# A ring of seven weight tiles, plain weights split two pairs at a time, and four pairs by seven products

## The chip, the cores and the metric

The kernel runs on one core of a Trainium2 chip. The metric is the device time of one execution in microseconds (us). Five engines work side by side and meet only through semaphores: TensorE (PE, with its weight loads shown as PEld), VectorE (DVE), ScalarE (ACT), GpSimd (POOL) and SyncE (SP), the last of which issues most of the DMA transfers.

## The reference

One decoder block on 256 tokens of width 2048, all in float32:

```python
h = h + 0.5 * swiglu(rms_norm(h, ffn1_norm), ffn1_w_gu, ffn1_w_down)
h = h + hybrid_mixer(rms_norm(h, mix_norm), w_in, ..., w_out)
h = h + 0.5 * swiglu(rms_norm(h, ffn2_norm), ffn2_w_gu, ffn2_w_down)
gate = sigmoid(rms_norm(h, ple_norm) @ ple_w_gate)
h = h + gate * (p @ ple_w_proj)
out = rms_norm(h, final_norm)

def swiglu(x, w_gu, w_down):
    gate, up = split(x @ w_gu, 2)
    return (silu(gate) * up) @ w_down
```

The hidden width of both feed-forward blocks (FFNs) is 5632. The mixer projects to 14 blocks of 512 columns, runs a gated delta rule and a stick-breaking attention on them, and projects back. Only the matrix products with large weights matter here.

## The kernel before

**Split products.** Every large product keeps float32 accuracy by splitting both operands into a high half (rounded to the matmul's input type) and a low half (the rest). A product of a 128x128 piece of the activations with a 128x512 piece of the weights is then three matmuls: high by high, high by low, low by high. Activations stand as the PE's stationary operand, weights move. The weights come from memory whole and are split on the chip: ACT casts the raw tile to the high half (`whi` or `shi`), then DVE subtracts it from the raw tile to give the low half (`wlo` or `slo`).

**Pairs.** The unit of plain work is a pair: two 128-row pieces of weights, 512 columns wide, 512 KB. `weight_pair` (L64) takes a `raw` tile (a ring of 4), a `whi` and a `wlo` tile (rings of 3 each), issues one load on SP's queue, one cast on ACT (L74) and one subtraction on DVE (L75). A pair feeds 12 matmuls (two pieces, two halves of the tokens, three matmuls each).

**Seven products.** Part of each FFN product is done by Strassen's scheme in its seven-product form: a 2x2 arrangement of weight blocks (two output blocks by the two halves of a pair's rows) against the 2x2 arrangement of the two halves of the tokens and of the rows. A `Group` (L245) covers two output blocks: gate and up of one hidden block of 512 columns (kind `gu`), or two blocks of the down projection (`dn`, `nb` 0 and 2), or two blocks of the last gate matrix (`behind`). Of each block's pairs the first `ns` go through the seven products, the others are plain. `ns` is `NS` = 4 for `gu`, `NS_DOWN` for `dn` (2, 3, 3 for the three parts), 2 for `behind`. The seven weight operands are made one after the other by `all_sums` (L287) from four loaded quarters `R`, 128 x (`ns` x 512): cast (L295), subtract (L296), then DVE or an accumulating DMA on POOL's queue (L311) adds the next quarter into `R`. `shi` and `slo` are rings of two. `product` (L324) runs one of the seven, 3 x `ns` matmuls; `halves` (L420) makes the sums and differences of the activations that the products need (`S`, `Sh`, `Sl`).

**Order.** The hidden blocks are worked in three `PARTS`: blocks 0 to 2, 3 to 6 and 7 to 10. For each part come its `gu` groups, then its two `dn` groups over the hidden blocks of this part. In the first FFN two hidden blocks are wholly plain, in the second one. `plan` (L351) writes the order of one FFN as a list: a group's plain pairs, and between them the seven products of the group that follows (from the second pair on where both are of one kind, from the third where they differ), so that the seven operands can be made while PE has other work. In the first `dn` group of a part the plain pairs that read the hidden block finished last stand at the end. All weights, of the mixer and the last stage too, form one list `order`. `next_weights` (L82) is called once for each piece of PE work; it issues splits ahead along that list, up to two pairs beyond the current one (`LEAD`) and up to two products' operands, and hands out the next one. Between pairs `lanes.step` advances small generators (norms, transposes, gating, `halves`).

**A hidden block's way.** `down_input` (L470) multiplies up by the gate's silu on DVE (L477), transposes blockwise (L482, `tb`), stores `tb` to memory and reads it back as `tT` (L488, L493), and splits it into `hTh` and `hTl` (ACT L499, DVE L500). For the last hidden block of a part the steps follow closer (`last`, L573).

**The end.** The last output block of the last gate matrix has its eight pairs split ahead into eight own buffers (L698), and its products run in two halves of the tokens.

The tile framework places each engine's instructions by its own order of readiness, with the program's order as priority; a tile waits until one of its tag's buffers is free.

## Time and profile before

| | us |
|---|---|
| median of 3 runs | 1951.76 |
| lowest, highest | 1951.52, 1951.91 |
| the profiled execution | 1953.25 |
| its span, first to last instruction | 1951.5 |

In the windows quoted below each row gives a stretch of the span and its length, then for PE, PEld, DVE, ACT and POOL the busy time with the number of instructions in brackets, then the granted PE clock, the DMA engines' busy share and what they moved in GB/s. In group rows the numbers behind the count are the total busy time, the mean duration in ns, and the engine's idle time just before the group with what ended it. In timeline rows the first number is the start in us, the second the time that the row covers. Rows of the chain give start, duration and what ran. A DMA issue row ends with the median time from issue to landing.

### The profile page before, as it was taken

How to read it: one execution, taken by the hardware profiler on the slowest of the kernel's cores; microseconds unless marked ns; L12 is line 12 of the kernel's file. 1: busy time of each engine (PE TensorE's matmuls, PEld its weight loads, DVE VectorE, ACT ScalarE, POOL GpSimd, SP SyncE). 2: the span in 40 equal slices, each digit the busy share in tenths (PEclk: the TensorE clock that was granted, in tenths of full speed). 3: DMA queues.
4: the chain of work that ended last, by engine and by line, in shares of the span. 5: the costliest groups of instructions: out<-in, count | busy, mean ns of one | idle time of the engine just before them, and what ended most of it. 6: DMA issues, size and time to landing. Idle time of an engine off the chain costs nothing.

```text
span 1951.5 us, 24163 instructions
## 1 busy us (share of the span) xinstructions
PE 1932.7 (99%) x8884; PEld 1591.6 (82%) x8884; DVE 1567.9 (80%) x1679; ACT 1163.1 (60%) x1358; POOL 148.8 (8%) x226
## 2 busy tenths in 40 slices
PE   9999999999999999999999999999999999999997
PEld 7888888888888888878788888888888788887886
DVE  7889878997889766797856579889888987888965
ACT  6656666566665567664555456566565755656653
POOL 0010100000010000010100000010000100001000
PEclk9999999999999999999999999999999999999999
DMA  8778888788887765556565786888898987988864
GB/s 311 268 238 276 255 288 285 227 293 251 282 283 237 225 216 172 175 169 209 173 201 160 244 289 226 226 285 289 241 282 251 303 266 237 272 255 282 249 208 141
DMA packets 144184, 475.06 MB, mean 243 GB/s; under 512 B 19649, under 2 KB 47297, under 8 KB 129857
## 3 DMA queue, kind: packets, MB, share of 16 engines
q1 hardware_dynamic: 107200, 302.16, 44.4%
q0 software_dynamic: 25920, 160.44, 30.2%
q10 hardware_dynamic: 10944, 10.91, 1.7%
q8 instruction: 69, 1.13, 0.2%
q14 instruction: 51, 0.41, 0.1%
HBM read 451.44 MB, written 22.02 MB: 243 GB/s over the span
## 4 chain that ended last, share of the span: by engine, by line
PE 87%; DVE 6%; DMA 4%; issue 2%; ACT 1%; SPq 0%; POOL 0%; POOLq 0%; DVEq 0%; ACTq 0%
PE g L340 5%; PE d L541 5%; PE d L542 5%; PE g L339 5%; PE d L540 4%; PE g L341 4%; PE u L540 4%; PE u L542 4%; PE u L541 4%; PE g L541 4%; PE g L542 4%; PE pj L109 4%; PE pj L110 4%; PE pj L111 4%; PE g L540 4%
## 5 line engine op out<-in xcount | busy, mean ns | idle before, releaser
L74 ACT CAST whi<-raw 128x1024 fp32r<-128x1024 f32 (+1 forms) x489 | 512.1, 1050 | 427.1 <-PE pj L111 109.9
L75 DVE TENSOR_TENSOR wlo<-raw,whi 128x1024 fp32r<-128x1024 f32 (+1 forms) x489 | 592.0, 1217 | 166.1 <-ACT whi L74 163.8
L296 DVE TENSOR_TENSOR slo<-R,shi 128x2048 fp32r<-128x2048 f32 (+2 forms) x224 | 445.2, 1989 | 149.0 <-ACT shi L295 147.6
L295 ACT CAST shi<-R 128x2048 fp32r<-128x2048 f32 (+2 forms) x224 | 374.2, 1671 | 140.5 <-DVE R L304 62.1
L109 PE MATMUL pj<-whi,nTh 128*128 128x512 f32 x448 | 179.4, 401 | 0.0
L110 PE MATMUL pj<-wlo,nTh 128*128 128x512 f32 x448 | 175.3, 391 | 1.1 <-DVE wlo L75 1.1
L111 PE MATMUL pj<-whi,nTl 128*128 128x512 f32 x448 | 174.9, 390 | 0.0
L541 PE MATMUL d<-wlo,hTh 128*128 128x512 f32 x448 | 174.3, 389 | 0.0
L540 PE MATMUL d<-whi,hTh 128*128 128x512 f32 x448 | 174.2, 389 | 0.0
L542 PE MATMUL d<-whi,hTl 128*128 128x512 f32 x448 | 173.7, 389 | 0.0
L541 PE MATMUL g<-wlo,nTh 128*128 128x512 f32 x400 | 155.9, 390 | 0.4 <-DVE wlo L75 0.4
L541 PE MATMUL u<-wlo,nTh 128*128 128x512 f32 x400 | 155.7, 389 | 0.5 <-DVE wlo L75 0.5
L542 PE MATMUL g<-whi,nTl 128*128 128x512 f32 x400 | 155.8, 390 | 0.0
L542 PE MATMUL u<-whi,nTl 128*128 128x512 f32 x400 | 155.7, 389 | 0.0
L540 PE MATMUL g<-whi,nTh 128*128 128x512 f32 x400 | 155.4, 390 | 0.0
L540 PE MATMUL u<-whi,nTh 128*128 128x512 f32 x400 | 154.2, 389 | 0.2 <-ACT whi L74 0.2
L304 DVE TENSOR_TENSOR R<-R 128x2048 f32<-128x2048 f32 (+2 forms) x68 | 135.7, 1995 | 0.1
L110 PEld LDWEIGHTS pj<-wlo,nTh 128*128 128x128 f32 x448 | 84.2, 188 | 18.9 <-DVE wlo L75 2.7
L111 PEld LDWEIGHTS pj<-whi,nTl 128*128 128x128 f32 x448 | 84.1, 188 | 17.6
L542 PEld LDWEIGHTS d<-whi,hTl 128*128 128x128 f32 x448 | 84.1, 188 | 17.6
L541 PEld LDWEIGHTS d<-wlo,hTh 128*128 128x128 f32 x448 | 84.1, 188 | 17.6
L540 PEld LDWEIGHTS d<-whi,hTh 128*128 128x128 f32 x448 | 84.1, 188 | 17.4
(332 smaller groups left out, 3445.2 us busy)
## 6 DMA issues: line engine op xcount, KB each, us to landing
raw<-in_w_gu SPq DMA_DIRECT2D x199, 512.0 KB, 5.7
raw<-in_w_down SPq DMA_DIRECT2D x112, 512.0 KB, 6.5
raw<-in_w_in SPq DMA_DIRECT2D x112, 512.0 KB, 3.4
R<-in_w_gu2q POOLq DMA_DIRECT2D x54, 1024.0 KB, 8.6
R<-in_w_gu1q POOLq DMA_DIRECT2D x48, 1024.0 KB, 8.6
raw<-in_w_out SPq DMA_DIRECT2D x32, 512.0 KB, 4.2
tT<-scr SPq DMA_DIRECT2D x22, 512.0 KB, 5.1
R<-in_w_down11q POOLq DMA_DIRECT2D x12, 768.0 KB, 6.0
```

Source lines behind the costliest of these rows:

```text
L74: nc.scalar.copy(hi[:, j, :], raw[:, j, :])
L75: nc.vector.tensor_tensor(out=lo[:, j, :], in0=raw[:, j, :], in1=hi[:, j, :], op=ALU.subtract)
L109: nc.tensor.matmul(outs[t], xh[:, c], whi[:, j, :], start=st, stop=False)
L110: nc.tensor.matmul(outs[t], xh[:, c], wlo[:, j, :], start=False, stop=False)
L111: nc.tensor.matmul(outs[t], xl[:, c], whi[:, j, :], start=False, stop=sp)
L295: keep(nc.scalar.copy(hi, w))
L296: nc.vector.tensor_tensor(out=lo, in0=w, in1=hi, op=ALU.subtract)
L304: keep(nc.vector.tensor_tensor(out=self.raw[x], in0=self.raw[x], in1=self.raw[y], op=ALU.add))
L339: nc.tensor.matmul(out, xh, whi[:, g, :], start=st, stop=False, skip_group_check=True)
L540: nc.tensor.matmul(out, xh[:, c], whi[:, j, :], start=st, stop=False, skip_group_check=True)
L541: nc.tensor.matmul(out, xh[:, c], wlo[:, j, :], start=False, stop=False, skip_group_check=True)
L542: nc.tensor.matmul(out, xl[:, c], whi[:, j, :], start=False, stop=sp, skip_group_check=True)
```

## The change

It does four things.

1. `NS_DOWN` becomes (2, 4, 3): the two down groups of the second part, in both FFNs, put four pairs through the seven products. `halves` gets a case for four pairs in a down group (one block of two, two of one), and `last` becomes 2 for this part.
2. The rings `whi`, `wlo` (3 each, one pair) and `shi`, `slo` (2 each, four pairs) become one ring of seven tiles of 128x2048, three in the pool that lives throughout (`w`) and four in the FFN's pool (`f`), in the order `ffwfwfw`. An operand of a product takes two of them, high and low.
3. From the third pair of each FFN up to its end (in the second FFN up to the `behind` group), plain pairs are split as quads: two pairs in one raw tile of 128x2048, loaded by two transfers, one cast and one subtraction, two tiles of the ring. All other plain pairs stay single: high and low side by side in one `w` tile. A quad's tiles are free again when both of its pairs have been used.
4. `raw` becomes a ring of two tiles of two pairs. Single pairs share one by twos, so both are loaded when the first is due. `next_weights` no longer counts pairs ahead; it issues as long as the oldest tiles of the ring that it needs have been used.

```diff
-LEAD = 2
+RING = "ffwfwfw"
+CAP = {x: RING.count(x) for x in "wf"}
...
-NS_DOWN = tuple(3 if i1 - i0 == 4 else 2 for i0, i1 in PARTS)
+NS_DOWN = (2, 4, 3)
...
-        raw = wp.tile([P, 2, NB], F32, tag="raw", name="raw", bufs=4)
-        hi = pool.tile([P, 2, NB], F32R, tag="whi", name="whi", bufs=bufs)
-        lo = pool.tile([P, 2, NB], F32R, tag="wlo", name="wlo", bufs=bufs)
...
+    def new_raw():
+        return wp.tile([P, 4, NB], F32, tag="raw", name="raw", bufs=2)
+
+    def halved(hi, lo, src):
+        nc.scalar.copy(hi, src)
+        nc.vector.tensor_tensor(out=lo, in0=src, in1=hi, op=ALU.subtract)
+
+    def weight_pair(raw, w, parts=1):
+        for i in range(parts):
+            j = slice(2 * i // parts, 2 * (i + 1) // parts)
+            halved(w[:, 0:2][:, j], w[:, 2:4][:, j], raw[:, j])
+        return w[:, 0:2], w[:, 2:4]
+
+    class Pairs:
+        def load(self):
+            if self.raw is None:
+                self.raw = new_raw()
+                n = 2 if done[0] else 1
+                for k in range(0, 2 * len(self.srcs), n):
+                    nc.sync.dma_start(out=self.raw[:, k:k + n], in_=self.srcs[k // 2][:, k % 2:k % 2 + n])
+            return self.raw
+
+    class Op:
+        def issue(self, where):
+            slots = [(wp if x == "w" else current[0]).tile([P, NS, NB], F32R, tag="w", name="w",
+                                                            bufs=CAP[x]) for x in where]
+            if self.kind == "sum":
+                self.out = [self.src.next_operand(*slots)]
+            elif self.kind == "single":
+                raw = self.src.load()[:, 2 * self.at:2 * self.at + 2]
+                self.out = [weight_pair(raw, slots[0], 2 if not done[0] else 1)]
+            else:
+                halved(slots[0], slots[1], self.src.load())
+                self.out = [tuple(x[:, 2 * i:2 * i + 2] for x in slots) for i in range(2)]
...
+    def places(op):
+        if op.kind == "single":
+            return "w"
+        return "".join(RING[(done[2] + i) % len(RING)] for i in range(2))
...
     def next_weights():
-        ahead = max(1, min(LEAD, done[1] // 2))
+        if done[1]:
+            uses[done[1] - 1][0].left -= 1
+        ahead = max(1, done[1] // 2)
...
+            if "f" in where and current[0] is None:
                 break
+            if any(len(ring[x]) + where.count(x) - CAP[x] > sum(not o.left for o in ring[x][:where.count(x)])
+                   for x in "wf"):
+                break
+            if sum(o.left > 0 for o in set(ring["w"] + ring["f"])) > ahead:
+                break
+            op.issue(where)
...
+    def add_plan(n):
+        first = len(order)
+        ffn_plan[n] = plan(n)
+        pairs = [i for i in range(first, behind_at.get(n, len(order))) if order[i][0] == "pair"][2:]
+        quads.update(pairs[:len(pairs) // 2 * 2])
...
-        for g0 in range(0, ns, 2):
-            n = min(2, ns - g0)
+        for g0, n in {1: ((0, 1),), 2: ((0, 2),), 3: ((0, 2), (2, 1)),
+                      4: ((0, 2), (2, 1), (3, 1)) if kind == "dn" else ((0, 2), (2, 2))}[ns]:
...
-                        last = (3 if i1 - i0 == 4 else 2) if len(hTh) == i1 else 0
+                        last = (6 - NS_DOWN[group.part] if i1 - i0 == 4 else 2) if len(hTh) == i1 else 0
...
-        ws = [weight_pair(a["w_pg"][3][g], fp, KD // 2) for g in range(KD // 2)]
+        ws = []
+        for g in range(0, KD // 2, 2):
+            both = Pairs([a["w_pg"][3][g], a["w_pg"][3][g + 1]])
+            for i in range(2):
+                w = fp.tile([P, 4, NB], F32R, tag="w", name="w", bufs=KD // 2)
+                ws.append(weight_pair(both.load()[:, 2 * i:2 * i + 2], w))
```

`next_operand` is the former `all_sums` with its two result tiles handed in. In the list of work (`make_program`) a quad stands at the place of its first pair.

More of the change, by code (lines that the diff above doesn't have):

```diff
@@ L82, in next_weights @@
-    def next_weights():
-        ahead = max(1, min(LEAD, done[1] // 2))
-        while done[0] < len(order):
-            kind, src = order[done[0]]
-            if kind != "load" and sum(k == kind for k, _ in split) > (ahead if kind == "pair" else 1):
-                break
-            done[0] += 1
-            if kind == "load":
-                src()
-            elif kind == "sum":
-                split.append((kind, next(src.sums)))
-            else:
-                split.append((kind, weight_pair(src, parts=2 if not done[1] and not split else 1)))
+            halved(w[:, 0:2][:, j], w[:, 2:4][:, j], raw[:, j])
@@ L96, in next_weights @@
         done[1] += 1
-        return split.pop(0)[1]
+        return op.out[i]
     def accumulate(outs, xs, nk):
@@ L265, in __init__ @@
                 self.plain.sort(key=lambda x: x[1] // 2)
-            self.sums = self.all_sums()
+            self.given = 0
         def new_banks(self):
@@ L399, in plan @@
             todo = []
+            if group.kind == "behind":
+                behind_at[n] = len(order)
             for j, (b, g) in enumerate(group.plain):
```

116 lines of the change are left out of this document (81 added, 35 removed).

## The prediction

> **What bounds the kernel now.** I read the page's engine shares first, then the chain that ended last, then busy time by windows, and last the single stretches in which PE isn't full.
>
> ```profile
> span 1951.5 us, 24163 instructions
> PE 1932.7 (99%) x8884; PEld 1591.6 (82%) x8884; DVE 1567.9 (80%) x1679; ACT 1163.1 (60%) x1358; POOL 148.8 (8%) x226
> PE 87%; DVE 6%; DMA 4%; issue 2%; ACT 1%; SPq 0%; POOL 0%; POOLq 0%; DVEq 0%; ACTq 0%
> ...
> 0.00:20.00 20.00, 18.25 (x77) 14.93 (x78) 13.34 (x23) 12.36 (x18) 0.79 (x7) 1.00 0.85 290
> ...
> 640.00:660.00 20.00, 19.27 (x85) 15.64 (x84) 16.13 (x14) 12.68 (x13) 0.88 (x1) 1.00 0.73 238
> ...
> 200.00:360.00 160.00, 160.00 (x707) 132.14 (x706) 134.55 (x103) 97.52 (x88) 15.92 (x24) 1.00 0.85 269
> ```
>
> PE is the bound: busy 99% of the span and 87% of the chain. In the middle of a feed-forward (FFN) block it never stops (160.00 us busy of 160, 707 matmuls, so 0.2263 us each). There DVE works 134.55 of 160 us (84%) and ACT 97.52 (61%), all of it beside PE. What is lost is lost at the edges: the first 20 us hold 77 matmuls and the change of part at 640 us 85, where a full 20 us (16.5 to 36.5, in a row below) hold 90. So only two things can move the time: the number of matmuls, and whether their weights are split in time at the places where little work lies ahead.
>
> **Part 1: four instead of three pairs by seven products.** A down group of the second part takes a fourth pair out of its plain list. That removes two plain pairs (one for each output block) of 12 matmuls, and adds three matmuls to each of seven products: 24 - 21 = 3 fewer. Two such groups in each of two FFNs: 12 matmuls x 0.2263 = **-2.7 us**, all on PE's path. Its split work:
>
> ```profile
> L75 DVE TENSOR_TENSOR wlo<-raw,whi 128x1024 fp32r<-128x1024 f32 x487 | 590.6, 1219 | 164.5 <-ACT whi L74 162.2 <-DMA tT<-scr 1.5
> L74 ACT CAST whi<-raw 128x1024 fp32r<-128x1024 f32 x487 | 510.8, 1052 | 425.6 <-PE pj L111 109.9 <-PE d L542 89.9 <-PE u L542 55.9
> L296 DVE TENSOR_TENSOR slo<-R,shi 128x2048 fp32r<-128x2048 f32 x133 | 304.4, 2289 | 116.4 <-ACT shi L295 115.6 <-DMA raw<-in_w_gu 0.6
> L295 ACT CAST shi<-R 128x2048 fp32r<-128x2048 f32 x133 | 254.5, 1914 | 108.8 <-DVE R L304 53.7 <-PE g L341 31.0 <-PE u L341 18.3
> L296 DVE TENSOR_TENSOR slo<-R,shi 128x1536 fp32r<-128x1536 f32 x56 | 98.2, 1755 | 22.7 <-ACT shi L295 22.3
> L304 DVE TENSOR_TENSOR R<-R 128x2048 f32<-128x2048 f32 x42 | 95.7, 2278 | 0.1
> L304 DVE TENSOR_TENSOR R<-R 128x1536 f32<-128x1536 f32 x16 | 27.9, 1742 | 0.0
> ```
>
> 28 products (seven in each of four groups) go from 1536 to 2048 wide: on DVE 28 x (2.289 - 1.755) = +15.0 us; eight pairs less: 8 x 1.219 = -9.8; the sums of R, eight of them, +8 x (2.278 - 1.742) = 4.3; one more block of input combinations, six operations in each FFN, none over the 0.64 us of the hTl row below, at most +7.7. That makes +17 us, spread over four groups with 16% of DVE free, so I cost it at nothing; without that cover it would be the 17 us. The quarter loads grow by 24 x 256 KB and the pair loads shrink by 8 x 512 KB: 2.1 MB more in all, hidden where the DMA share is 0.85.
>
> The part has a price in order, though. In the group's plain list the last four pairs read the hidden block that was gated last. Before, 2 + 5 products of nine matmuls and six pairs (135 matmuls, 30.6 us) lie between the end of that block's up-projection and its first reader; after, 2 + 3 products of twelve and four pairs (108, 24.4 us). The chain to the finished block, from the first gating to the end of the last low half:
>
> ```profile
> 375.87 0.75 DVE L477 SCALAR_TENSOR_TENSOR sil<-u,rstd,sil 128x512 f32<-128x512 f32 x1
> ...
> 398.94 1.28 DVE L500 TENSOR_TENSOR hTl<-tT,hTh 128x512 fp32r<-128x512 f32 x2
> 1522.44 0.75 DVE L477 SCALAR_TENSOR_TENSOR sil<-u,rstd,sil 128x512 f32<-128x512 f32 x1
> ...
> 1546.61 1.29 DVE L500 TENSOR_TENSOR hTl<-tT,hTh 128x512 fp32r<-128x512 f32 x2
> 635.16 9.91 DMA tT<-scr
> ```
>
> 24.3 us in the first FFN, 25.5 in the second. Six microseconds of slack become none: late by 0 and 1.1 us, **+1.0 us**. Below, 0 (a product can be pulled ahead); above, about 5 (both loads of tT as slow as the 9.91 us at 635, and ACT's queue standing behind the casts that wait for it).
>
> **Part 2: plain pairs two at a time.** FFN pairs are 199 + 1 + 112 = 312; less 8, less the two singles at the start of each FFN, 300 make 150 quads. One cast and one subtraction of 2048 replace two of 1024: DVE 150 x (2 x 1.219 - 2.289) = -22 us, ACT 150 x (2 x 1.052 - 1.914) = -29 us. Neither lies on PE's path in the windows above, so I count nothing for it. The Trainium skill, Perfetto Trace Analysis, section Optimizing Scalar/DVE Operations, says grouping into larger operations helps a saturated engine, while breaking instructions up lets work finish sooner where Scalar or Vector aren't saturated but hold up others. The 84% and 61% of the window row put this kernel in the second case; by the first case the sum would be only the -2.7 us, without the terms that follow.
>
> What a quad adds is latency: PE can't start it before both loads have landed and a cast of 1.914 (not 1.052) is done. That matters where PE runs close behind the loads.
>
> *First quad.* Today:
>
> ```profile
> 10.47 1.05 ACT L74 CAST whi<-raw 128x1024 fp32r<-128x1024 f32 x1 [0.34 <-DMA raw<-in_w_gu]
> 11.82 1.05 ACT L74 CAST whi<-raw 128x1024 fp32r<-128x1024 f32 x1 [0.30 <-DMA raw<-in_w_gu]
> ...
> 12.14 0.61 PE L540 MATMUL g<-whi,nTh 128*128 128x512 f32 x2
> 12.93 0.73 PE L540 MATMUL u<-whi,nTh 128*128 128x512 f32 x2 [0.17 <-ACT whi L74]
> 13.50 0.39 PE L541 MATMUL g<-wlo,nTh 128*128 128x512 f32 x1
> ```
>
> The third pair is cast at 10.47, the fourth at 11.82, when its load has landed. Together they start at 11.82 and are ready at 13.73, 1.6 us after PE's 12.14. The four matmuls from 12.14 to 13.50 now lose 1.36 - 0.91 = 0.45 there, so **+1.2 us**, with the 16 matmuls on high halves (3.6 us) covering the subtraction of 2.289, as the rows show PE doing now. Bounds: 0, and +3.2 if the low half is awaited at once (16.02).
>
> *The raw ring.* Four raw tiles of one pair become two of two pairs. In a stretch of plain pairs alone (11 quads in the first FFN's first two groups) a tile must be loaded, cast and subtracted within the two quads before it comes round, 48 x 0.2263 = 10.9 us.
>
> ```profile
> 16.50:36.50 20.00, 20.00 (x90) 16.57 (x89) 18.31 (x28) 17.36 (x33) 0.00 (x0) 1.00 1.00 372
> ...
> raw<-in_w_gu SPq DMA_DIRECT2D x9, 512.0 KB, 5.7
> ...
> R<-in_w_gu1q SPq DMA_DIRECT2D x4, 1024.0 KB, 9.8
> ```
>
> A pair lands in 5.7 us (20 to 45 us); its twin behind it needs 512 KB at 372 GB/s, 1.4 more. 7.1 + 1.914 + 2.289 = 11.3 us, 0.4 too long, for five rounds: **+2.2 us**. Below: 5.7 alone gives 9.9 us and no loss. Above: 1 MB in 9.8 us, the R loads' row, gives 14.0 and 5 x 3.1 = 15.7 us. I take the first, since it is the same transfer. The Trainium skill, DMA: Bandwidth & Descriptors, section Anatomy of one DMA, fits about 2.0 us plus bytes at 436 GB/s, 4.4 us for 1 MB; with that figure the round would take 8.6 us and this term would be zero. The measured 9.8 us for 1 MB in this stretch disagrees with it.
>
> *Start of the second FFN.* Its pairs come behind four R loads of 1 MB:
>
> ```profile
> 1158.74 12.33 DMA raw<-in_w_gu
> 1171.17 1.06 ACT L74 CAST whi<-raw 128x1024 fp32r<-128x1024 f32 x1 [0.47 <-DMA raw<-in_w_gu]
> 1172.39 1.06 ACT L74 CAST whi<-raw 128x1024 fp32r<-128x1024 f32 x1 [0.16 <-DMA raw<-in_w_gu]
> 1173.54 0.50 PE g L541
> ```
>
> PE already waits there (the chain runs through this load). As a quad the two start at 1172.39 and are ready at 1174.30 instead of 1172.23: **+2.1 us**. Bounds: 0 if the ring has a quad in hand, +3.1 with the low half.
>
> *The end.* The last block's eight pairs stay single but load through the two raw tiles.
>
> ```profile
> 1914.05 5.37 DMA raw<-in_w_pg
> 1921.57 5.16 DMA raw<-in_w_pg
> 1926.75 1.06 ACT whi L74
> 1927.84 1.24 DVE wlo L75
> 1929.12 0.50 PE gt L122
> ```
>
> The eighth pair's load starts when the fourth is split (1921.57). Then the seventh starts there too, and its subtraction stands before the eighth's: **+1.2 us**. Bounds: -0.8 (all of the present wait) and +4 (both rounds pay it, and the second landing 1.4).
>
> In the mixer the order of splits doesn't change, only odd pairs load a place earlier; nothing, with 1 us to either side.
>
> **Sum.** -2.7 + 1.0 + 1.2 + 2.2 + 2.1 + 1.2 = **+5.0 us**. The profiled execution took 1953.25 us (span 1951.5 and 1.75 around it), 1.5 above the median; to the median of 1951.76 the sum gives **1956.8 us**, 0.26% slower.
>
> **Rivals.** *The covers hold:* rings of seven tiles give up to three and a half quads ahead, loads arrive in time, and only matmuls and end count, -2.7 + 0 to 1.2: about 1950. For it: no PE stop at all in the 160 us row. Against: the rows at 12.93 and 1173.54.
>
> *Faster, at the part changes.* There PE waits for a copy that stands in ACT's queue behind casts:
>
> ```profile
> PE d L339 <- ACT part L347: 2.7, 4, 0.7
> ```
>
> If 29 us less of casts on ACT shorten that queue, these 2.7 us go too and the starts cost nothing: -5.4, 1946.4. It decides once the cast of tT no longer stands ahead of the copy. Against it: that cast waits for a DMA, which the change doesn't hasten.
>
> *Slower, the ring itself.* Quads and products share seven tiles in turn. If a tile is taken strictly in turn, a quad's low half waits for the tile of the quad before, free only one product before its use. I count 85 such quads from the plan's lists (three of a group's four where products and pairs alternate from the second pair, two where the first product comes a pair later): 12 with a product of two as the cover, 10 of three, 63 of four. With one matmul more the cover is 1.58, 2.26 and 2.94 us against 2.289. That costs 12 x 0.71 = 8.5 us plus 0.3, and with DVE at 84% the 0.65 us left at the 63 can go as well (0.5 us each, 31 us). I price it at +9 on top: 1966. Tiles given out as any comes free leave a whole pair more; I take that as likelier.
>
> **How the numbers follow.** Chances: forecast (1953 to 1962) 0.42, covers hold 0.22, faster at the part changes 0.14, strict ring 0.22. A measurement of this kernel tells about 0.2% (3.9 us) from no change. Within it lie 0.12 of the forecast's case and 0.20 of the covers': same 0.32. Faster: 0.14 + 0.02 = 0.16. Slower: 0.30 + 0.22 = 0.52. The range goes from the faster rival's 1946 to 1968, just above the strict ring's price; the slower cases alone have 1955 to 1968.
>
> **What would show it.** PE's matmuls: 8872. A PE gap before the third pair near 13.7 us, and near 1174. The raw loads in pairs, landing over 7 us in the first 60 us. The hidden block's casts beside a PE wait at about 400 and 1547 us. The strict ring would show as many short PE waits for the low halves of plain weights (0.1 to 0.7 us) in the windows that are full now. If those windows stay full and the starts don't grow, the forecast is wrong toward 1950.

## The result: 77.5 us slower

| | before | after |
|---|---|---|
| median, us | 1951.67 (1951.52 to 1951.91, 4 runs) | 2029.18 (2027.58 to 2032.74, 4 runs) |
| ratio | 1 | 1.04, 95% interval 1.0381 to 1.0418 |
| span of the profiled execution, us | 1951.5 | 2025.9 |

The forecast of 1956.8 us and its range up to 1968 missed by far; the sign alone was right. The page of the kernel after, its span, engine shares and chain:

```profile
span 2025.9 us, 23629 instructions
PE 1951.3 (96%) x8872; PEld 1592.1 (79%) x8872; DVE 1574.9 (78%) x1533; ACT 1143.5 (56%) x1202; POOL 149.3 (7%) x226
PE 71%; DVE 13%; DMA 7%; issue 4%; ACT 4%; SPq 0%; ACTq 0%; POOL 0%; DVEq 0%; POOLq 0%
```

PE has its 12 matmuls less (8872). But it holds only 71% of the chain (before 87%), DVE 13% (6%). ACT lost 156 instructions and 20 us of work, DVE 146 instructions, though not its time. An engine with less to do made PE wait more. The same stretches as in the prediction, and two more (columns as there):

```profile
0.00:20.00 20.00, 15.95 (x60) 12.43 (x61) 13.72 (x22) 13.31 (x20) 0.79 (x7) 0.91 0.84 289
200.00:360.00 160.00, 154.23 (x675) 125.92 (x674) 129.23 (x79) 93.52 (x69) 15.87 (x24) 1.00 0.84 264
380.00:400.00 20.00, 16.40 (x63) 12.57 (x64) 16.29 (x17) 12.80 (x14) 1.99 (x3) 0.91 0.82 230
640.00:660.00 20.00, 19.32 (x84) 15.37 (x83) 14.70 (x15) 12.86 (x14) 3.07 (x5) 1.00 0.90 274
1200.00:1220.00 20.00, 12.78 (x46) 9.39 (x45) 11.56 (x13) 7.12 (x5) 0.00 (x0) 0.83 0.77 309
```

The stretch that was full has 675 matmuls instead of 707: 32 x 0.2263 = 7.2 us gone where the prediction counted nothing. The first 20 us have 60 instead of 77, the stretch from 380 us 63 (89 before), the start of the second FFN 46 (87 before). Only the stretch at 640 us is as it was. These are stretches of the clock, and the kernel after runs ever further behind: by the count of matmuls it reaches the work of before's 250 us at 270 us and that of 400 us at 431, and its second FFN starts at 1193.39 us instead of 1155.45. So for that start the row of before from 1160 us is the one to compare:

```profile
380.00:400.00 20.00, 20.00 (x89) 16.43 (x89) 19.82 (x18) 12.90 (x14) 2.33 (x3) 1.00 0.89 260
1160.00:1180.00 20.00, 19.81 (x87) 16.07 (x87) 17.72 (x23) 12.82 (x14) 0.80 (x1) 1.00 0.91 350
```

To see where the 74 us between the two spans are, I took each 512-wide matmul's start and the next matmul's start, and summed what lies over 226.7 ns:

| stretch, us | before | after |
|---|---|---|
| 0 to 100, start | 2.9 | 8.2 |
| 100 to 250, first change of part | 1.3 | 15.6 |
| 300 to 450, second part's change | 1.4 | 12.0 |
| 550 to 650, third part's change | 2.1 | 6.1 |
| 700 to 1150, mixer | 12.5 | 14.0 |
| 1150 to 1250, start of the second FFN | 0.9 | 11.1 |
| 1250 to 1450 | 1.4 | 12.0 |
| 1500 to 1650 | 2.3 | 10.2 |
| 1700 to 1950 | 2.6 | 11.0 |
| whole span | 27.9 | 104.6 |

76.7 us more, less 2.7 for 12 matmuls: 74.0, the difference of the spans (74.4). It is spread over every start and change of part of both FFNs. What PE waited for, the largest rows of the waits view of after (sum in us, times, longest; L418 to L420 are now the products' matmuls, L636 to L638 those of plain pairs, L554 and L426 the copies `Sh` and `part`, L70 and L392 the casts):

```profile
PE d L418 <- ACT Sh L554: 9.5, 4, 3.0
PE g L418 <- ACT part L426: 8.5, 6, 1.5
PE d L418 <- ACT part L426: 8.0, 6, 3.4
PE g L636 <- ACT w L70: 6.6, 3, 5.9
PE g L637 <- DVE w L71: 4.5, 4, 1.9
PE u L637 <- DVE w L71: 3.2, 5, 1.5
PE d L637 <- DVE w L71: 3.1, 6, 0.9
```

Before, the largest row of that kind in an FFN was the 2.7 us that the prediction quotes. What stands first now are small copies on ACT. ACT was idle for 44% of the span, so it was not too slow for them: they stood behind a cast that waited. The same view for ACT, before and then after:

```profile
ACT shi L295 <- DVE R L304: 62.1, 29, 6.2
```

```profile
ACT w L392 <- DVE R L380: 208.1, 56, 7.8
ACT w L70 <- DMA raw<-in_w_gu: 45.5, 21, 7.3
```

A product's cast waits for the sum of the quarters on DVE 56 times instead of 29, and a quad's cast for its load 21 times. Whatever ACT has to do next waits with it.

### The profile page after: what moved, and what is told of

The parts are those of the page before. It is cut to its first block, busy times and chain, and to the rows that moved or that the text cites. A ratio compares the mean times of both kernels' runs of the same rounds, so it can differ in the third digit from the quotient of the medians.

```text
span 2025.9 us, 23629 instructions
## 1 busy us (share of the span) xinstructions
PE 1951.3 (96%) x8872; PEld 1592.1 (79%) x8872; DVE 1574.9 (78%) x1533; ACT 1143.5 (56%) x1202; POOL 149.3 (7%) x226
## 3 DMA queue, kind: packets, MB, share of 16 engines
q0 software_dynamic: 25920, 166.74, 29.3%
## 4 chain that ended last, share of the span: by engine, by line
PE 71%; DVE 13%; DMA 7%; issue 4%; ACT 4%; SPq 0%; ACTq 0%; POOL 0%; DVEq 0%; POOLq 0%
DVE w L71 4%; PE pj L194 4%; PE pj L195 4%; PE pj L196 4%; PE u L637 4%; PE u L638 4%; PE g L418 4%; PE g L419 4%; PE g L420 4%; PE u L636 3%; DMA raw<-in_w_gu 3%; PE g L637 3%; PE g L638 3%; PE g L636 3%; PE d L637 3%
## 5 line engine op out<-in xcount | busy, mean ns | idle before, releaser
L71 DVE TENSOR_TENSOR w<-raw,w 128x1024 fp32r<-128x1024 f32 (+2 forms) x331 | 562.5, 1702 | 257.2 <-ACT w L70 179.1
L70 ACT CAST w<-raw 128x1024 fp32r<-128x1024 f32 (+2 forms) x331 | 475.5, 1438 | 340.9 <-PE pj L196 101.4
L392 ACT CAST w<-R 128x2048 fp32r<-128x2048 f32 (+2 forms) x224 | 385.0, 1725 | 318.3 <-DVE R L380 208.1
L393 DVE TENSOR_TENSOR w<-R,w 128x2048 fp32r<-128x2048 f32 (+2 forms) x224 | 458.4, 2052 | 114.0 <-ACT w L392 72.8
L194 PE MATMUL pj<-w,nTh 128*128 128x512 f32 x448 | 179.6, 401 | 0.0
L195 PE MATMUL pj<-w,nTh 128*128 128x512 f32 x448 | 175.4, 392 | 1.2 <-DVE w L71 1.2
L196 PE MATMUL pj<-w,nTl 128*128 128x512 f32 x448 | 174.9, 390 | 0.0
L637 PE MATMUL d<-w,hTh 128*128 128x512 f32 x416 | 164.3, 395 | 3.3 <-DVE w L71 3.1
L638 PE MATMUL d<-w,hTl 128*128 128x512 f32 x416 | 163.0, 393 | 0.0
L636 PE MATMUL g<-w,nTh 128*128 128x512 f32 x400 | 156.1, 393 | 6.6 <-ACT w L70 6.6
L637 PE MATMUL g<-w,nTh 128*128 128x512 f32 x400 | 157.8, 395 | 4.5 <-DVE w L71 4.5
L636 PE MATMUL d<-w,hTh 128*128 128x512 f32 x416 | 161.0, 393 | 0.2 <-ACT w L70 0.2
L637 PE MATMUL u<-w,nTh 128*128 128x512 f32 x400 | 157.0, 393 | 3.3 <-DVE w L71 3.2
L638 PE MATMUL g<-w,nTl 128*128 128x512 f32 x400 | 156.8, 392 | 0.0
L638 PE MATMUL u<-w,nTl 128*128 128x512 f32 x400 | 156.1, 390 | 0.0
L636 PE MATMUL u<-w,nTh 128*128 128x512 f32 x400 | 153.1, 391 | 2.7 <-ACT w L70 2.7
L195 PEld LDWEIGHTS pj<-w,nTh 128*128 128x128 f32 x448 | 84.2, 188 | 19.2 <-DVE w L71 3.0
L637 PEld LDWEIGHTS d<-w,hTh 128*128 128x128 f32 x416 | 78.8, 189 | 23.6 <-DVE w L71 7.3
L194 PEld LDWEIGHTS pj<-w,nTh 128*128 128x128 f32 x448 | 84.2, 188 | 16.7
L636 PEld LDWEIGHTS g<-w,nTh 128*128 128x128 f32 x400 | 75.5, 189 | 23.2 <-ACT w L70 7.6
```

Of the source, the lines that this page charges most:

```text
L70: nc.scalar.copy(hi, src)
L71: nc.vector.tensor_tensor(out=lo, in0=src, in1=hi, op=ALU.subtract)
L194: nc.tensor.matmul(outs[t], xh[:, c], whi[:, j, :], start=st, stop=False)
L195: nc.tensor.matmul(outs[t], xh[:, c], wlo[:, j, :], start=False, stop=False)
L196: nc.tensor.matmul(outs[t], xl[:, c], whi[:, j, :], start=False, stop=sp)
L392: keep(nc.scalar.copy(hi, w))
```

## The experiments

Theories at the start: **width** (casts and subtractions of 2048 make others wait, and come late themselves), **raw** (two raw tiles of two pairs load too late), **four** (the fourth pair makes the part changes late), and **ring** (quads and products from seven common tiles have too short a head start). All kernels were run beside the kernel before. Differences are of medians.

| run | what it is | us | ratio, 95% interval |
|---|---|---|---|
| e1 | before, four pairs by seven products | +15.6 | 1.0082 (1.0065 to 1.0098) |
| e2 | after, three pairs | +69.9 | 1.0358 (1.0342 to 1.0373) |
| e3 | after, quads cast and subtracted by pair | +46.1 | 1.0235 (1.022 to 1.0251) |
| e4 | after, no quads, own rings | +35.2 | 1.0178 (1.0163 to 1.0194) |
| e5 | e3, four raw tiles of one pair | +39.8 | 1.0203 (1.0186 to 1.022) |
| e6 | e1, eight sums on POOL | +29.3 | 1.0151 (1.0136 to 1.0166) |
| e7 | before, 18 us more on DVE at the changes | +7.1 | 1.0038 (1.0023 to 1.0053) |
| e8 | before, the same in mid-part | +2.4 | 1.0014 (1.0005 to 1.0024) |
| e9 | ring of seven, single pairs, four pairs | +14.5 | 1.0075 (1.006 to 1.009) |
| e10 | e5, no further ahead than before | +40.6 | 1.0206 (1.0191 to 1.0221) |
| e11 | before, sums issued one later | -0.9 | 0.9996 (0.9987 to 1.0006) |
| e12 | e9, three pairs | +25.7 | 1.013 (1.0113 to 1.0146) |
| e13 | e5, second pair split in its own place | +42.4 | 1.022 (1.0205 to 1.0235) |
| e14 | before, splits in the quads' order | +0.7 | 1.0003 (0.9993 to 1.0012) |
| e15 | after, subtraction by pair, cast whole | +58.3 | 1.0306 (1.0284 to 1.0328) |
| e16 | e1, products one place earlier | +16.4 | 1.0084 (1.0067 to 1.0101) |
| e17 | e9, six tiles | +32.9 | 1.0164 (1.0149 to 1.018) |
| e18 | e5, three pairs | +34.9 | 1.0179 (1.0162 to 1.0196) |

### The parts of the change: e1 to e5

e1, with the pieces in which `halves` makes the combinations and `last` as after:

```diff
-NS_DOWN = tuple(3 if i1 - i0 == 4 else 2 for i0, i1 in PARTS)
+NS_DOWN = (2, 4, 3)
```

> The kernel before with four pairs by seven products in the second part's down groups and nothing else of the change: pairs cast one at a time, rings of their own, raw tiles of one pair. 12 matmuls fewer than before. Theories that put the 77 us into the weights' ring or into wide casts expect -3 to +2 us against before (the 2.7 us of matmuls, and up to 5 us back at the part changes). The theory that the fourth pair makes the hidden block's halves late at each part change expects +20 us or more, with PE stops behind the small sums Sh at 380, 640, 1520 and 1780 us.

e2, in the kernel after:

```diff
-NS_DOWN = (2, 4, 3)
+NS_DOWN = (2, 3, 3)
```

> The kernel after with three pairs by seven products as before: ring of seven, pairs two at a time, raw tiles of two pairs. 12 matmuls more than after. Theories that put the loss into the ring, the wide casts or the raw tiles expect +70 to +82 us against before. The theory of the fourth pair expects +55 us or less.

e3, in the kernel after:

```diff
-                halved(slots[0], slots[1], self.src.load())
+                raw = self.src.load()
+                for i in range(2):
+                    j = slice(2 * i, 2 * i + 2)
+                    halved(slots[0][:, j], slots[1][:, j], raw[:, j])
```

> The kernel after, with each cast and each subtraction of two plain pairs cut into two of 1024 elements; tiles, ring, loads and order stay. If the width of the instructions makes PE wait (a small operation or a product's cast stands behind 1.9 and 2.3 us of work, and the first pair is late), it falls to +0 to +20 us against before. If the ring is the cause (a tile of two pairs is held for two pairs' matmuls, so that a product's operand can start only some 3 us before its use), the order of the work on DVE and ACT is the same and most remains: +50 to +80 us.

e4, in the kernel after:

```diff
-        return "".join(RING[(done[2] + i) % len(RING)] for i in range(2))
+        return "ff"
...
-        quads.update(pairs[:len(pairs) // 2 * 2])
```

> The kernel after with plain pairs one at a time: they take the three tiles of the weights' pool, a product's operand takes two of the other four tiles, as before the change; raw tiles of two pairs and four pairs by seven products stay. If the shared ring and the pairing cause the loss, it goes back to -3 to +5 us against before. If the raw tiles of two pairs cause a part of it (late loads at the start of each feed-forward block), +5 to +25 us remain, at 0 to 100 and near 1205 us. If the fourth pair does, +20 us or more remain at the part changes.

None of the four theories has it alone: e1 and e3 lie between the ranges that their theories gave, e4 lies above the one for the raw tiles, and e2's 69.9 only just misses the one for ring, width and raw tiles together. The fourth pair costs 15.6 us by itself and 7.6 on top of the ring (77.5 - 69.9). Cutting the wide instructions takes 31.4 us away (77.5 - 46.1), and that is the largest single part. e4 stands 19.6 us above e1, and its main difference from e1 is the raw tiles. What a late load does is plain in ACT's timeline of e4 (start, time covered; then line, operation, tiles and the wait before it):

```profile
363.20 0.62 ACT L553 CAST Sh<-S 128x512 fp32r<-128x512 f32 x1 [0.29 <-DVE S L551]
371.23 1.04 ACT L70 CAST w<-raw 128x1024 fp32r<-128x1024 f32 x1 [7.41 <-DMA raw<-in_w_down]
372.18 0.61 ACT L553 CAST Sh<-S 128x512 fp32r<-128x512 f32 x1
```

In e1 the same cast started at 366.99 and the same `Sh` at 367.95: there each pair has a raw tile of its own. In e4 a cast of 1.04 us waits 7.41 us for its load, the `Sh` behind it is 4.2 us late, and PE stops for it. Nothing in this chain is busy.

e5 takes that out of the kernel with quads: four raw tiles of one pair, and quads cast pair by pair.

```diff
-        return wp.tile([P, 4, NB], F32, tag="raw", name="raw", bufs=2)
+        return wp.tile([P, 2, NB], F32, tag="raw", name="raw", bufs=4)
```

> The run with quads cast pair by pair (+46 us against before), with raw tiles as before the change: four of one pair, each loaded on its own. Ring of seven, quads and four pairs stay. If the raw tiles of two pairs cost their own share (the run without quads stood 20 us above the run with the four pairs alone, with ACT waiting for late loads in front of the sums' casts), it falls by 15 to 25 us, to +21 to +31 us. If in the kernel with quads the ring alone holds the loads back, it stays at +40 to +46 us.

It gained 6.3 us, not 15 to 25: a miss. The 20 us of e4 are not what the raw tiles cost under quads; two late things that end at the same time aren't paid twice.

### What the fourth pair costs: e6, e7, e8, e16

e6, in e1's `all_sums`:

```diff
-                keep(nc.vector.tensor_tensor(out=self.raw[x], in0=self.raw[x], in1=self.raw[y], op=ALU.add))
+                eng = nc.gpsimd if self.kind == "dn" and self.part == 1 else nc.vector
+                keep(eng.tensor_tensor(out=self.raw[x], in0=self.raw[x], in1=self.raw[y], op=ALU.add))
```

> The run with the four pairs alone (+15.6 us against before), with two in-place sums of the quarters in each of the second part's down groups (8 in all, 2.28 us each on DVE) computed on POOL, which is 8% busy. Theory that a saturated DVE at the part changes is the cause: 18 us of work leave DVE there, +2 to +10 us remain. Rival, that it is the chain of the hidden block or the serial chain of the products (which a slower POOL makes longer): +15 us or more.

e7 and e8 add to the kernel before, in `all_sums`, and set `more` for other groups: `p == 1` of the down groups, or `i in (5, 6)` of the gate and up groups.

```diff
                 nc.vector.tensor_tensor(out=lo, in0=w, in1=hi, op=ALU.subtract)
+                if self.more:
+                    nc.vector.tensor_tensor(out=lo[:, 0], in0=w[:, 0], in1=hi[:, 0], op=ALU.subtract)
```

> The kernel before, with one more DVE subtraction of 128x512 (some 0.65 us, the same values written again) behind each of the 28 products of the second part's down groups: 18 us of DVE work, no matmul more or less, no order changed. If DVE has no time to spare at the part changes, whatever its mean over the block, it is slower by +8 to +18 us. If the mean of 84% tells what is free there, 0 to +3 us.

> The same 28 subtractions behind the 28 products of the second part's last two gate and up groups, whose operands are made in the middle of the part, where DVE works some 83% of the time. If place decides, -1 to +3 us against before. If 18 us of DVE work cost the same anywhere, as much as the run with them at the part changes.

The same 28 subtractions (19.0 us of DVE work) cost 7.1 us at the changes of part and 2.4 in mid-part. The intervals of the two touch (1.0023 to 1.0053, 1.0005 to 1.0024), so that the place decides a part of the price is likely, not certain; and 7.1 lies under the 8 to 18 that the theory of a full DVE asked for, and well under the 18.3 us that e1 lost beside its matmuls (15.6 + 2.7). The place where it costs is one that the prediction's mean had hidden. The kernel before in windows of 10 us (the third number with a count behind it is DVE's busy time):

```profile
330.00:340.00 10.00, 10.00 (x46) 8.29 (x45) 7.35 (x6) 6.55 (x6) 1.08 (x2) 1.00 0.90 326
340.00:350.00 10.00, 10.00 (x45) 8.27 (x45) 10.00 (x12) 3.25 (x3) 0.89 (x1) 1.00 0.55 130
...
380.00:390.00 10.00, 10.00 (x45) 8.28 (x45) 10.00 (x10) 5.03 (x5) 0.89 (x1) 1.00 0.78 192
390.00:400.00 10.00, 10.00 (x45) 8.15 (x44) 9.82 (x9) 7.87 (x9) 1.45 (x2) 1.00 1.01 329
400.00:410.00 10.00, 10.00 (x46) 8.29 (x45) 9.79 (x10) 6.19 (x6) 1.64 (x3) 1.00 1.02 381
```

From 380 to 410 us DVE has 0.39 us free of 30, in a block whose mean is 84%. PE is still full: the stock of split weights covers it.

But DVE's load isn't the whole price. e6 took 18 us from DVE and became 13.7 us slower than e1. The group on POOL, and what PE waited for (first two rows of the waits view of e6):

```profile
L305 POOL TENSOR_TENSOR R<-R 128x2048 f32<-128x2048 f32 x8 | 38.6, 4821 | 41.2 <-DVE slo L296 41.2
```

```profile
PE d L341 <- DVE slo L296: 10.3, 4, 4.1
PE g L545 <- DVE wlo L75: 9.6, 6, 4.3
```

A sum takes 4.82 us there instead of 2.28, and PE waits for the product behind it and for a plain pair's low half that stands in DVE's queue behind that. Cast, subtraction and sum of one quarter follow each other, and the next product's cast waits for the sum; with four pairs that chain is 1.91 + 2.29 + 2.28 = 6.5 us, of which 2 x 0.53 in subtraction and sum are new. In this run the chain's length counted more than DVE's load. The Trainium skill, Perfetto Trace Analysis, section Optimizing Scalar/DVE Operations, says that work may be moved from a saturated DVE to GPSIMD, with the reserve that the two share a port; here the duration of the moved sum, in a serial chain, was enough to lose.

e16, in e1's `plan`, moves the down group's products one place ahead:

```diff
-                    1 if group.kind == follower.kind else 2
+                    0 if group.part == 1 and group.kind == follower.kind == "dn" else \
+                    1 if group.kind == follower.kind else 2
```

> The run with the four pairs alone (+15.6 us), where in the second part's first down group each product goes one place ahead in the list of plain pairs, so that 12 more matmuls (2.7 us) lie in front of the four pairs that read the last hidden block. If that block's late halves are the main price (stops of 2.9 and 3.2 us, and 1.9 us each of matmuls at the lower clock behind them), it falls to +2 to +9 us. If the products' own operands are late there, they are later by one place: +15 us or more.

Its largest PE wait, beneath the two largest of e1:

```profile
PE d L543 <- ACT hTh L502: 5.8, 2, 3.1
PE d L339 <- ACT shi L295: 4.1, 4, 1.1
```

```profile
PE d L544 <- ACT hTh L503: 7.4, 2, 3.9
```

The wait for the last hidden block, which the prediction had named, is there in e1: 5.8 us in two stops. With 12 more matmuls ahead of it in the list it did not shrink but grew. So the matmuls ahead aren't its measure; that the block's cast is as late as the products' splits that share its queue is the likelier reading, and no run shows it. In e1's trace this block's share can be counted: from one matmul's start to the next the two stops are 2.9 and 3.2 us, and behind each come 1.9 us of slow matmuls (last section), about 10 of the 18.3 us in all. The other 8 are mostly waits for the products' operands and for low halves, and of the size of e7's 7.1. Whether the 10 us would come back if the block were in time, no run shows.

### The ring: e9 to e14, e17, e18

e9 gives a plain pair one tile with both halves in it, split in its own place and given back after its own matmuls:

```diff
             elif i in quads:
-                if quad is None:
-                    quad = Op("quad", Pairs([src]), 0, 2)
...
+                op = Op("any", Pairs([src]))
+                program.append(op)
+                uses.append((op, 0))
```

> The run with quads and four raw tiles (+40 us against before), without the quads: each plain pair takes one tile of the ring of seven (high and low half in it), is cast where its turn comes and gives its tile back after its own matmuls; products take two tiles, four pairs by seven products stay. If the quads cost the 24 us between that run and the one with the four pairs alone (two pairs stand together ahead of a product's operand, and hold two tiles until both are used), it falls to +12 to +22 us. If the shared ring costs them (weights and products run out of each other's tiles, or weights run ahead and stand in front of small operations), it stays at +32 us or more.

e10 adds to e5's `next_weights`, ahead of `op.issue`:

```diff
+            if sum(u[0].kind == "sum" and op.kind == "sum" or u[0].kind != "sum" and op.kind != "sum"
+                   for u in uses[done[1]:] if u[0].out) > (1 if op.kind == "sum" else 2):
+                break
```

> The run with quads and four raw tiles (+40 us), in which no weights are split further ahead than before the change: a quad starts only when at most two pairs wait for their matmuls, a product's operand when at most one does. If the quads' run ahead is what puts casts in front of products and small operations, it falls to +15 to +28 us. If pairing as such, with a tile held for two pairs, costs the 24 us, it stays at +36 to +45 us.

e11, in the kernel before:

```diff
-sum(k == kind for k, _ in split) > (ahead if kind == "pair" else 1)
+sum(k == kind for k, _ in split) > (ahead if kind == "pair" else 0)
```

> The kernel before, with one thing changed: a product's operand is begun only when the one before it has been taken by its product, so one is under way instead of two. No instruction more or less. It measures what the head start of the products is worth by itself. If a product's chain (cast 1.9, subtraction 2.3, sum 2.3 us) needs that start, it is slower by 30 us or more, with PE stops in front of products all along both feed-forward blocks. If there is start enough without, +0 to +8 us.

e12 is e9 with `NS_DOWN = (2, 3, 3)`.

> The ring of seven with single pairs, with three pairs by seven products as before: of the change only the shared ring is left. If the ring alone is harmless, -3 to +3 us against before (a version that could beat both); if the shared ring costs, +15 us or more. By the run with the four pairs alone, it should stand some 16 us below the ring with single pairs and four.

Single pairs in the ring stand 25 us below quads (e9 against e5), so with four pairs the quads are the price and the common ring isn't. Working the list less far ahead (e10, e11) changes nothing. But e12 missed on the other side: with three pairs the ring alone costs 25.7 us. Its largest PE wait:

```profile
PE u L419 <- ACT Sh L555: 9.1, 3, 3.8
```

ACT's timeline of e12 ahead of one of these stops, and of before at the same place:

```profile
419.60 2.00 ACT L70 CAST w<-raw 128x1024 fp32r<-128x1024 f32 x2 [6.22 <-DMA raw<-in_w_down]
...
423.40 1.91 ACT L393 CAST w<-R 128x2048 fp32r<-128x2048 f32 x1
...
439.23 1.90 ACT L393 CAST w<-R 128x2048 fp32r<-128x2048 f32 x1 [4.21 <-DVE R L381]
441.03 0.58 ACT L424 COPY g<-g 128x512 f32<-128x512 f32 x1
441.55 1.04 ACT L555 CAST Sh<-S 128x1024 fp32r<-128x1024 f32 x1
```

```profile
410.01 1.91 ACT L295 CAST shi<-R 128x2048 fp32r<-128x2048 f32 x1 [0.98 <-PE d L341]
...
431.58 1.92 ACT L295 CAST shi<-R 128x2048 fp32r<-128x2048 f32 x1
433.86 1.06 ACT L74 CAST whi<-raw 128x1024 fp32r<-128x1024 f32 x1 [0.37 <-ACT shi L295]
436.19 1.05 ACT L460 CAST Sh<-S 128x1024 fp32r<-128x1024 f32 x1 [1.27 <-DVE S L458]
```

e12 is by then 4.7 us behind, so the clock times can't be compared as they stand; the order can. In both kernels the same product's cast stands ahead of `Sh`. In e12 it waits 4.21 us for a sum on DVE, `Sh` stands behind it, and PE stops 3.16 us for `Sh`. The cast isn't early: the products' chain is late. The operand two before it was cast at 423.40 us in e12, behind a plain pair's cast that had waited 6.22 us for its load, and at 410.01 before; PE was 40 matmuls further on (1822 against 1782). Three more plain pairs had been cast ahead of it (102 against 99). So here the ring puts plain pairs, and their loads, in front of the operand that PE needs. This is read from one stop; why the ring costs less with four pairs (14.5) than with three (25.7) stays open.

Two causes were left for the quads: the order of their splits, or the two tiles that stay locked until both pairs are used. e13 splits the second pair in its own place, but keeps the tiles:

```diff
-                for i in range(2):
-                    j = slice(2 * i, 2 * i + 2)
-                    halved(slots[0][:, j], slots[1][:, j], raws[i])
+                halved(*self.out[0], raws[0])
...
+                    program.append(("second", quad.second))
```

> The run with quads and four raw tiles (+40 us), in which a quad still takes its two tiles at the first pair's place and gives them back after the second's matmuls, but the second pair's cast and subtraction are issued at that pair's own place, behind the product's operand that lies between. If the order is the cause (two pairs' casts and subtractions stand in front of a product's operand in the queues of ACT and DVE, and two products' operands then follow each other, the second waiting for the first one's sum), it falls to +12 to +24 us. If the tiles held for two pairs are the cause, it stays at +34 to +42 us.

e14 does the opposite in the kernel before: a second pair is put behind its first in the list of splits, and nothing else.

```diff
+            if i in quads and first is not None:
+                program.insert(first + 1, i)
+                first = None
+                continue
```

> The kernel before with nothing but the order of the weights' splits changed: of the plain pairs that make a quad after the change, the second is loaded, cast and subtracted directly behind the first. Rings, raw tiles, widths, three pairs by seven products as before; the matmuls stand in the order of before. If the order is the cause: +15 to +30 us. If it is the tiles: -2 to +6 us.

Order costs nothing (e14) and its repair gains nothing (e13). e17, in e9, takes stock away without quads:

```diff
-RING = "ffwfwfw"
+RING = "fwfwfw"
```

> The ring with single pairs and the four pairs (+14.5 us against before), with six tiles instead of seven: less split weight in stock ahead of PE, and nothing else. If stock is what counts (quads lock tiles for two pairs and cost 25 us that way), one tile less costs +8 to +30 us more: +22 to +45 us against before. If the seven tiles hold more than is needed, it stays at +12 to +18 us, and the tiles that quads lock can't be their price.

e18 is e5 with `NS_DOWN = (2, 3, 3)`.

> The run with quads and four raw tiles with three pairs by seven products as before. With four pairs, the quads stood 25 us above single pairs in the ring (+40 against +14.5); the ring with single pairs and three pairs stood at +25.7. If the quads' price adds to whatever the ring costs: +45 us or more. If ring and quads pay for the same stops: +28 to +40 us.

The largest PE wait of e17, in two stops at changes of part, is for a product's operand (2.0 us in e9):

```profile
PE d L419 <- ACT w L393: 10.4, 2, 5.8
```

One tile of seven less costs 18.4 us (32.9 - 14.5; the order of the two pools changes with it). So the stock of tiles is what this kernel lives on at its changes of part, and a quad, which keeps two until 24 matmuls are done, lives on less of it. That the locked tiles are the quads' price is argued from what is left over (e13, e14) and from the price of a tile (e17), not shown by a run that takes the lock alone away. One rival is left: `next_weights` goes on only when the oldest tiles that it needs have been used, so a locked quad also holds back free tiles that come after it in turn, and no run gives tiles out in another order. And the price isn't a constant: 25.3 us with four pairs, 9.2 with three (34.9 - 25.7), where the ring had already been paid for.

### The wide instructions: e15

```diff
-                halved(slots[0], slots[1], self.src.load())
+                raw = self.src.load()
+                nc.scalar.copy(slots[0], raw)
+                for j in (slice(0, 2), slice(2, 4)):
+                    nc.vector.tensor_tensor(out=slots[1][:, j], in0=raw[:, j], in1=slots[0][:, j], op=ALU.subtract)
```

> The kernel after (+77.5 us) with one cast over both pairs of a quad as it has it, but a subtraction for each pair. With both cut by pair it stood at +46. If the 31 us between come from the wide subtraction on DVE, the busier engine, it falls to +44 to +55; if from the wide cast on ACT (the first pair's high half waits for both loads and 1.9 us), it stays at +65 to +78.

It lies between the two: 19.2 of the 31.4 us go with the subtraction (77.5 - 58.3), 12.2 with the cast (58.3 - 46.1). I matched casts, subtractions and first matmuls of the first FFN's plain pairs in order: between the end of a subtraction and the first matmul that reads its low half lie 5.1 us in the median before. For pairs that are the first of a quad (in the kernel before: of the same two) it is 4.7 us before, 3.5 in e3 and 2.7 in the kernel after, which differs from e3 by the width alone; a quarter of them lie under 3.0, 1.6 and 0.7 us. For the second ones it is 5.5, 6.0 and 6.1. So the width takes from the first pair, all along the block and not only at the starts, and nothing from the second.

## Why the prediction was wrong

**The matmuls** were right: 8872, 2.7 us.

**"16% of DVE free, so I cost it at nothing"** is the first step that failed. The four pairs alone lost 18.3 us beside their matmuls (e1: 15.6 + 2.7). That this is near the 17 us that the prediction gave for the case without cover is luck: about 10 of it are the hidden block's stops and what follows them, which were another term, and 19.0 us of DVE work in the same places cost 7.1 (e7). So by these numbers the term was worth some 8 us, not 0 and not 17. 84% was the mean over a stretch of 160 us; at the part change from 380 to 410 us DVE has under 2% to spare. e7 and e8 point to the place; e6 points to the longer serial chain besides DVE's load.

**"Neither lies on PE's path in the windows above, so I count nothing for it"** is the second and the larger: 31 us for casts and subtractions of 2048. The prediction saw that a quad adds latency, and looked for it only where PE runs close behind the loads. PE was full in the windows before while low halves lay ready some 5 us ahead of it; a full PE says that this reserve was enough, not how much of it was left over. The second case of the Trainium skill, Perfetto Trace Analysis, section Optimizing Scalar/DVE Operations (breaking instructions up helps where they hold up others), which the prediction quoted, is what e3 shows, with 31.4 us.

**"Tiles given out as any comes free leave a whole pair more; I take that as likelier"** is the third. The change's own text decides it the other way: `next_weights` goes on only when the oldest tiles have been used, so tiles are taken in turn. The rival of the ring had the right sign, and a part of its mark came: waits for the low halves of plain weights in windows that were full, in the kernel after 10.8 us in 15 waits at L637, the longest 1.9. It was priced at +9, and the 31 us that it named for 63 more quads were left out; the ring with quads by pair and four raw tiles shows +24 to +35 (e5 against e1, and e18). The lock of two tiles for 24 matmuls was no part of it, and no run parts lock and turn.

**The hidden block's chain, +1.0**, was mis-sized: about 10 us in e1, of which 5.8 stand in the waits view, where about 5 was the upper bound. In the kernel after it doesn't show, since PE there waits before that for `Sh` and `part`.

**The starts.** The first quad: 17 matmuls fewer in the first 20 us, 3.8 us, where +1.2 was taken and 3.2 the upper bound. The low half was awaited after all: the prediction counted on 16 matmuls on high halves to cover its subtraction "as the rows show PE doing now", but the rows show four (12.14 to 13.50). The first low half was used at 15.98 us instead of 13.50, 2.5 us later (which is also what the prediction's own 16.02 gives, not 3.2); the rest is slow matmuls behind the stop. Start of the second FFN: +2.1 at 1174 us, which is 18 us after that FFN's first matmul. In the kernel after that place is at 1212 us, and a stop of 5.93 us ends there; the stretch of the table loses 10.2 us in all. Place and cause were right, the size was not. ACT's timeline of after shows the wait, with two things in it:

```profile
1207.07 1.04 ACT L554 CAST Sh<-S 128x1024 fp32r<-128x1024 f32 x1 [4.39 <-DVE S L552]
1209.80 1.90 ACT L70 CAST w<-raw 128x2048 fp32r<-128x2048 f32 x1 [1.68 <-DMA raw<-in_w_gu]
```

and SP's queue why the load was late: it was issued behind four loads of 1 MB and waited for a raw tile of two pairs.

```profile
1193.63 2.01 SPq L361 DMA_DIRECT2D R<-in_w_gu2q  x4
1195.75 19.10 SPq L91 DMA_DIRECT2D raw<-in_w_gu  x6
```

The raw ring's mechanism was right, its place wrong: it costs where a load stands behind other loads and ACT's queue behind the load (e4), not in the stretch of plain pairs alone. It wasn't a term to add: 19.6 us without quads, 6.3 with them. The fit of the Trainium skill that the prediction set beside this term (DMA: Bandwidth & Descriptors, section Anatomy of one DMA) is given there for transfers issued by GpSimd; these loads were issued by SP, so their 9.8 us neither confirm nor refute it.

**The end, +1.2**, did not come: by the measure of the table the last 75 us lose 0.2 us, 1.0 before. That is its lower bound, -0.8.

**The sum itself** was built of places where PE already waited before. The parts that cost most lay where PE did not wait yet, and those prices overlap: e1, e9, e5, e3 and after stand at 15.6, 14.5, 39.8, 46.1 and 77.5, but by way of three pairs the same steps are 25.7, 34.9 and 69.9. Which part pays for a stop depends on what else ends there, so no one table of prices holds. No run was faster than the kernel before beyond its interval; e11 (0.9996) is the same time.

## What to carry to other kernels

A bound engine that is always busy lives on a stock of finished operands: before an edit is costed at nothing, measure how long operands lie ready before they are used, and look at the helpers' load in windows about as short as that stock lasts (here some 5 us; windows of 10 us showed it), not over a whole stage. Merging two units of work halves the instructions, but also makes both wait for the later input, holds both buffers until the later use, and makes everything behind them in the same queue wait for both. Where a cast that heads an engine's queue waits for a transfer or a sum, the small operation behind it pays (7.41 us of waiting, `Sh` 4.2 us late, in e4).

## What the hardware showed besides

PE's clock fell after stops. e4's timeline of PE at its stop near 1181 us:

```profile
1185.03 1.22 PE L635 MATMUL g<-w,nTh 128*128 128x512 f32 x2 [4.30 <-ACT w L70]
...
1187.31 0.63 PE L636 MATMUL g<-w,nTh 128*128 128x512 f32 x1
1187.73 0.63 PE L637 MATMUL g<-w,nTl 128*128 128x512 f32 x1
...
1191.14 0.39 PE L636 MATMUL g<-w,nTh 128*128 128x512 f32 x1
1191.37 0.39 PE L637 MATMUL g<-w,nTl 128*128 128x512 f32 x1
```

From 1.9 us after the restart matmuls start 0.42 us apart instead of 0.23, for some 4 us; the window from 1180 to 1200 us had a granted clock of 0.83 and that from 1160 to 1180 1.00. In the traces of all twenty kernels I counted the stops in front of a 512-wide matmul and asked whether at least four of the next 24 matmuls started 0.40 to 0.45 us apart: so it was behind all 18 stops of over 3.4 us, 17 of 19 between 2.5 and 3.4, and 17 of 30 between 1.8 and 2.5. The Trainium skill, TensorE: Matmul & The Clock Gate, Part 1, says that the clock is halved after an idle window of about 3.4 us; the rate nearly agrees (0.23 to 0.42 us), but stops of 1.8 to 3.4 us were often enough here, and the slow stretch begins after the stop is over. In the kernel after some 30 matmuls ran so, about 6 us of its 74: a stop is dearer than its length.
